# A second token mixer whose scores are laid over all four 64x64 tiles of the matmul array

## The chip, the cores and the metric

The kernel runs as one program on one core of a Trainium2 chip. The metric is the device time of one execution in microseconds (us). Engines are named as in the profile: PE is the matmul engine (TensorE), PEld its loading of weights, DVE is VectorE, ACT is ScalarE, POOL is GpSimd, SP starts most of the transfers. Each engine works through its own queue strictly in the order in which the program was laid out; a waiting instruction holds up everything behind it on its engine.

## The reference, cut to what matters

Two layers are computed for 256 frames of one prompt and 8 streams of 16 frames (samples). Each layer is SwiGLU block, token mixer, SwiGLU block, each followed by a layer norm. The change touches only the mixer of the second layer: grouped-query attention with 16 query heads, 4 key/value heads of 64 elements, rotary positions, and a learned "sink" per query head that takes part in the softmax as one more score without a value:

```python
def _attend(q, k, v, valid, bias, sinks):
    s = jnp.einsum("bqhgd,bkhd->bhgqk", q, k, ...) * (HEAD_DIM ** -0.5)
    ...
        sk = sinks.astype(jnp.float32)[None, :, :, None, None]
        m = jnp.maximum(jnp.max(s, axis=-1, keepdims=True), sk)
        e = jnp.exp(s - m)
        p = e / (jnp.sum(e, axis=-1, keepdims=True) + jnp.exp(sk - m))
    return jnp.einsum("bhgqk,bkhd->bqhgd", p.astype(v.dtype), v)
```

A prompt frame reads its own chunk of 64 frames and the two chunks before it; a sample frame reads 128 cached keys and the 16 of its own stream.

## The kernel before, in words

All activations stay in the core's memory, and the weights stream through a ring. A dense product in near-full precision is three matmuls (`mm3`, lines 193 to 195), high part times high part and two mixed ones. The second mixer (`mixer_b`) runs these stages: `m.natural` three times (the projections to the first half of the queries, to keys and values, to the second half of the queries), then `m.finish` (the output projection: 8 steps `k` of the contraction for each of 3 tiles `t` of frames, six dense matmuls each). The attention of 8 pairs of heads for the prompt (`prompt(c)`) and of 8 units of two streams (`sample(b, g)`) is cut into pieces by Python generators, and a small planner (`Flow`) puts the pieces between the dense matmuls. Each `yield` says how much PE time the piece costs, how long to wait before the next, which PSUM banks and buffers it keeps and which the next piece needs; `room` caps them. `finish` calls `flow.until(("p", k))` before it uses head pair `k`. Behind the planner a scheduler sets the final order of each engine's queue.

One unit of the prompt before: 8 score matmuls (line 983) with 64 rows of contraction and 64 columns of output, on the two tiles of the array that lie on its diagonal (row group r writes column group r); a softmax (reductions on DVE at line 991, exponentials on ACT at 994 and 999, scaling on DVE at 1005); six transposes (1011) copied out by ACT (`pTp`, 1014); four matmuls with v (1022); and ACT and DVE split the result into high and low parts (`xh`, `xl`, lines 71 and 72), from which the output projection reads it. One unit of the samples: four score matmuls (1037), softmax (1042 to 1058), four transposes (1062, 1064) copied out half by ACT (`pT`, 1068) and half by DVE (1069), eight matmuls with v (1078), and two copies to `oTs` (1084). The sinks are loaded once by four small transfers on POOL's queue (`load_sinks`, 875 and 878).

Of the kernel before, what the change touches and what calls it, by code (L numbers as in the profile page):

```python
# [45 lines left out]
def encoder_step(ctx, tc, a, o):  # L46
# [822 lines left out]
    def load_sinks():  # L869
        sinks = const.tile([P, 2], F32, name="sinksb")  # L870
        sinkp = const.tile([P, 8], F32, name="sinkpb")
        sk = a["sinks"]
        with nc.allow_non_contiguous_dma(reason="a few sinks"):
            for g in range(2):
                nc.gpsimd.dma_start(
                    sinks[:, g:g + 1], bass.AP(sk.tensor, sk.offset + 8 * g, [[1, 8], [0, DS], [1, 1]])
                )
                nc.gpsimd.dma_start(
                    sinkp[:, 4 * g:4 * g + 4],
                    bass.AP(sk.tensor, sk.offset + 8 * g, [[4, 2], [0, 64], [1, 4]]),  # L880
                )
        return sinks, sinkp
# [8 lines left out]
    def mixer_b(sunk, cache):  # L891
        with ExitStack() as st:
# [5 lines left out]
            nsinks = m.mp.tile([P, 2], F32, name="nsinksb")  # L898
            nc.vector.tensor_scalar(nsinks, sinks, -1.0, None, op0=ALU.mult)
            nsinkp = m.mp.tile([P, 8], F32, name="nsinkpb")  # L900
            nc.vector.tensor_scalar(nsinkp, sinkp, -1.0, None, op0=ALU.mult)


            sps = [m.mp.tile([P, 6 * P], F32, name=f"sp{i}b") for i in range(3)]
# [71 lines left out]
            def prompt(c):  # L976
                g = c // 4
                pks = [bank(), bank()]
                for u, (i, a0, a1, _) in enumerate(bands):
                    k0 = 64 if u == 3 else 0  # L980
                    for r in range(2):
                        w = slice(64 * r, 64 * r + 64)
                        nc.tensor.matmul(  # L983
                            pks[i][w, a0:a1], qT[w, c, 64 * u:64 * u + 64], kT[w, g, k0:k0 + a1 - a0],
                            start=True, stop=True,
                        )
                nm = stp.tile([P, 4], F32, name="nm4")
                sm = stp.tile([P, 4], F32, name="sm4")
                sp = sps[c % 3]
# [16 lines left out]
                yield 1.0, 3.82, {"bank": 2, "sp": 1}, {"bank": 2, "pTp": 1}  # L1006
                pT = m.m2.tile([P, 6, 2, 64], F32, name="pTp")
                for h, js in enumerate(((0, 1, 2, 4), (3, 5))):
                    pt = bank()
                    for i, j in enumerate(js):  # L1010
                        nc.tensor.transpose(  # L1011
                            out=pt[:, i * P:(i + 1) * P], in_=sp[:, j * P:(j + 1) * P], identity=ident
                        )
                    nc.scalar.copy(
                        pT[:, 4 * h:4 * h + len(js)].rearrange("p j r q -> p (j r q)"), pt[:, 0:len(js) * P]
                    )
                yield 0.65, 0.65, {"bank": 2, "pTp": 1}, {"bank": 1}
                po = bank()
                for t, js in enumerate((slice(0, 4), slice(4, 6))):
                    for r in range(2):  # L1020
                        w = slice(64 * r, 64 * r + 64)
                        nc.tensor.matmul(  # L1022
                            po[w, t * P:SEQ].rearrange("p (u q) -> p u q", q=64),
                            v[:, t, P * g + 64 * r:P * g + 64 * r + 64], pT[:, js, r, :],
                            start=(t == 0), stop=(t == 1),
                        )
                m.put_prompt(c, po[:, 0:SEQ])
# [3 lines left out]
            def sample(b, g):  # L1031

                pk = bank()[:, 0:2 * n].rearrange("p (i k) -> p i k", i=2)
                for i in range(2):
                    for r in range(2):
                        w = slice(64 * r, 64 * r + 64)
                        nc.tensor.matmul(  # L1037
                            pk[w, i, :], qs[w, g, b + i].rearrange("p j q -> p (j q)"), kc[w, b + i, g, :],
                            start=True, stop=True,
                        )  # L1040
                nm = stp.tile([P, 2], F32, name="nm")
                nc.vector.tensor_reduce(nm, pk, axis=AX.X, op=ALU.max, negate=True)
                nc.vector.tensor_scalar(nm, nm, nsinks[:, g:g + 1], None, op0=ALU.min)
                s = m.m3.tile([P, 2, n], F32, name="s")
                sm = stp.tile([P, 2], F32, name="sm")
                for i in range(2):
                    nc.scalar.activation(
                        s[:, i], pk[:, i], AF.Exp, bias=nm[:, i:i + 1], accum_out=sm[:, i:i + 1]
                    )
                es = stp.tile([P, 2], F32, name="es")  # L1050
                nc.scalar.activation(es, nm, AF.Exp, bias=sinks[:, g:g + 1])
# [7 lines left out]
                yield 0.5, 3.5, {"bank": 1, "s": 1}, {"bank": 1, "pT": 1}  # L1059
# [12 lines left out]
                for i in range(2):  # L1072
                    for l in range(2):
                        for r in range(2):
                            w = slice(64 * r, 64 * r + 64)
                            u = slice((2 * l + i) * P + 64 * r, (2 * l + i) * P + 64 * r + 64)
                            d = slice(P * g + 64 * r, P * g + 64 * r + 64)
                            nc.tensor.matmul(  # L1078
                                po[w, i, :], v[:, 2, d] if l else vc[:, b + i, d],
                                pT[:, u], start=(l == 0), stop=(l == 1),  # L1080
                            )
# [5 lines left out]
            def add_p(c):  # L1087
                flow.add({("k", 0), ("k", 1), ("q", 0, c), ("q", 1, c)}, {"bank": 2, "sp": 1}, prompt(c))

            def add_s(b, g):  # L1090
                flow.add({("k", 2)} | {("q", 2, 4 * g + j) for j in range(4)}, {"bank": 1, "s": 1}, sample(b, g))
# [153 lines left out]
```

## Time and profile before

| | us |
|---|---|
| median of 3 runs | 1419.72 (1419.4 to 1421.39) |
| profiled execution, its own time | 1419.12 |
| its span, from the first to the last instruction | 1417.4 |
| PE busy | 1404.8 (99%) |
| DVE busy | 1052.0 (74%) |
| ACT busy | 644.7 (45%) |
| POOL busy | 49.1 (3%) |

The span is what the trace covers; the execution's own time is 1.7 us longer. PE is busy nearly throughout, but matmuls overlap each other in the pipeline, so the length of a piece of PE work is read from the start of its first instruction to the start of what follows it, not from the sum of durations. The mixer's attention lies between about 1048 and 1125 us of the span.

### The profile page before, as it was taken

The page shows a single profiled execution, that of the slowest core. Times are in us where ns is not written, and L with a number is a line of the kernel's source. Part 1 is how long each engine was busy: PE and PEld are TensorE (multiplying, and loading weights), DVE is VectorE, ACT ScalarE, POOL GpSimd, SP SyncE. Part 2 cuts the span into 40 slices and gives each one's busy share as a digit, 9 for nine tenths or more (in the row PEclk, how much of TensorE's full clock was granted, in tenths as well). Part 3 has the DMA queues.
Part 4 walks back from the last instruction along what each step waited for, and adds up shares of the span by engine and source line. Part 5 has one row for each costly group of instructions (what it writes and reads, how often), then busy time and mean ns, then how long its engine had stood idle before and what let it go on. Part 6 is the DMA issues. An engine that isn't in the chain of part 4 may idle for free. (4 is left out here: it accounts for less than half of the span.)

```text
span 1417.4 us, 21251 instructions
## 1 busy us (share of the span) xinstructions
PE 1404.8 (99%) x8048; PEld 1270.9 (90%) x8048; DVE 1052.0 (74%) x1912; ACT 644.7 (45%) x1201; POOL 49.1 (3%) x72
## 2 busy tenths in 40 slices
PE   9999999999999999999999999999999999999997
PEld 8999999898887899999989999999787789999996
DVE  6877877755356787787777778786967788778775
ACT  6544444256564544444425444443346554444440
POOL 1110000100000000000000000000100000000001
PEclk9999999999999999999999999999999999999999
DMA  7645334375845543433425363433241164343321
GB/s 278 241 132 152 119 119 158 119 232 182 289 142 194 189 140 105 149 119 120 160 97 174 104 208 119 135 97 123 96 166 61 52 208 141 107 148 119 119 74 45
DMA packets 68693, 203.19 MB, mean 143 GB/s; under 512 B 6844, under 2 KB 19648, under 8 KB 68464
## 3 DMA queue, kind: packets, MB, share of 16 engines
q1 hardware_dynamic: 63344, 187.72, 39.7%
q0 software_dynamic: 2944, 10.71, 2.4%
q10 hardware_dynamic: 2304, 3.41, 0.6%
q8 instruction: 63, 1.03, 0.3%
q14 instruction: 38, 0.31, 0.1%
HBM read 196.56 MB, written 5.24 MB: 142 GB/s over the span
## 5 line engine op out<-in xcount | busy, mean ns | idle before, releaser
L193 PE MATMUL bank<-xh,ring_h 128*128 128x384 f32 x1440 | 486.5, 338 | 0.0
L195 PE MATMUL bank<-xh,ring_l 128*128 128x384 f32 x1440 | 483.5, 336 | 0.0
L194 PE MATMUL bank<-xl,ring_h 128*128 128x384 f32 x1440 | 482.4, 335 | 0.0
L72 DVE TENSOR_TENSOR ring_l<-raw,ring_h 128x1024 fp32r<-128x1024 f32 (+2 forms) x258 | 300.1, 1165 | 217.3 <-ACT ring_h L71 213.4
L71 ACT CAST ring_h<-raw 128x1024 fp32r<-128x1024 f32 (+2 forms) x258 | 258.2, 1003 | 400.4 <-PE bank L194 197.0
L193 PEld LDWEIGHTS bank<-xh,ring_h 128*128 128x128 f32 x1440 | 270.7, 188 | 8.7 <-issue 1.2
L194 PEld LDWEIGHTS bank<-xl,ring_h 128*128 128x128 f32 x1440 | 270.8, 188 | 6.7 <-DVE ring_l L72 0.5
L195 PEld LDWEIGHTS bank<-xh,ring_l 128*128 128x128 f32 x1440 | 270.5, 188 | 0.0
L71 ACT CAST ring_h<-wd 128x512 fp32r<-128x512 f32 x216 | 133.6, 619 | 103.4 <-PE bank L194 81.3
L371 DVE TENSOR_TENSOR x<-x,bank 128x512 f32<-128x512 f32 x236 | 160.5, 680 | 17.9 <-PE bank L195 16.9
L72 DVE TENSOR_TENSOR ring_l<-wd,ring_h 128x512 fp32r<-128x512 f32 x216 | 148.1, 686 | 13.8 <-ACT ring_h L71 13.8
L195 PE MATMUL bank<-ring_h,hl 128*128 128x512 f32 x348 | 137.6, 395 | 0.0
L193 PE MATMUL bank<-ring_h,hh 128*128 128x512 f32 x348 | 137.2, 394 | 0.0
L194 PE MATMUL bank<-ring_l,hh 128*128 128x512 f32 x348 | 136.8, 393 | 0.0
L193 PE MATMUL bank<-ring_h,xh 128*128 128x512 f32 x288 | 118.2, 410 | 0.0
L194 PE MATMUL bank<-ring_l,xh 128*128 128x512 f32 x288 | 113.3, 393 | 0.1
L195 PE MATMUL bank<-ring_h,xl 128*128 128x512 f32 x288 | 112.9, 393 | 0.0
L195 PEld LDWEIGHTS bank<-ring_h,hl 128*128 128x128 f32 x348 | 65.4, 188 | 15.7 <-DVE hl L72 0.8
L194 PEld LDWEIGHTS bank<-ring_l,hh 128*128 128x128 f32 x348 | 65.4, 188 | 12.5
L193 PEld LDWEIGHTS bank<-ring_h,hh 128*128 128x128 f32 x348 | 65.8, 189 | 11.9
L193 PEld LDWEIGHTS bank<-ring_h,xh 128*128 128x128 f32 x288 | 54.2, 188 | 13.8 <-issue 3.7
L195 PEld LDWEIGHTS bank<-ring_h,xl 128*128 128x128 f32 x288 | 54.1, 188 | 11.8 <-DVE xl L72 0.2
(195 smaller groups left out, 1425.6 us busy)
## 6 DMA issues: line engine op xcount, KB each, us to landing
raw<-in_w_in SPq DMA_DIRECT2D x172, 512.0 KB, 3.3
wd<-in_w_down SPq DMA_DIRECT2D x72, 512.0 KB, 4.3
raw<-in_w_down SPq DMA_DIRECT2D x16, 512.0 KB, 3.2
kta<-in_kT_a SPq DMA_DIRECT2D x16, 512.0 KB, 6.4
vca<-in_v_a SPq DMA_DIRECT2D x16, 512.0 KB, 6.9
raw<-in_w_qk_a SPq DMA_DIRECT2D x16, 512.0 KB, 3.7
raw<-in_w_qkv_b SPq DMA_DIRECT2D x12, 512.0 KB, 3.5
raw<-in_w_v_a SPq DMA_DIRECT2D x8, 512.0 KB, 4.2
```

The source lines that it names most:

```text
L71: cast = nc.scalar.copy(hi, src)
L72: nc.vector.tensor_tensor(lo, src, hi.bitcast(F32), op=ALU.subtract)
L193: nc.tensor.matmul(out, lh, rh, start=first, stop=False, skip_group_check=partial)
L194: nc.tensor.matmul(out, lh, rl, start=False, stop=False, skip_group_check=partial)
L195: nc.tensor.matmul(out, ll, rh, start=False, stop=last, skip_group_check=partial)
L371: nc.vector.tensor_tensor(z, z, sums[b], op=ALU.add)
```

## The change

Scores of the prompt are computed for two pairs of heads (c and c+1) in one piece, those of the samples for the two streams of a unit. For the second of the two, row group r of the array writes column group 1-r. So the four 64x64 tiles are all addressed, and the two score matrices go to different PSUM banks. The second one then has its heads' rows swapped, which is why sinks are loaded in both orders (16 small transfers for 4), why the sink's exponential of a sample takes an addition on DVE first, and why the matmuls with v read the swapped half (`r ^ x`). A piece of the prompt now holds four banks and two of four `sp` buffers, and the numbers that it tells the planner are others. `soften` is the softmax of one pair of heads as it was.

```diff
-                room = {"bank": 6, "sp": 3, "s": 3, "pTp": 2, "pT": 2, "qr": 2}
+                room = {"bank": 6, "sp": 4, "s": 3, "pTp": 2, "pT": 2, "qr": 2}
...
+                for i in range(2):
+                    for r in range(2):
+                        w = slice(64 * (r ^ i), 64 * (r ^ i) + 64)
+                        at = sk.offset + 8 * g + 4 * r
+                        nc.gpsimd.dma_start(sinks[w, g, i:i + 1], bass.AP(sk.tensor, at, [[1, 4], [0, DS], [1, 1]]))
+                        nc.gpsimd.dma_start(sinkp[w, g, :, i], bass.AP(sk.tensor, at + i, [[0, 64], [2, 2]]))
...
             def prompt(c):
                 g = c // 4
-                pks = [bank(), bank()]
+                pks = [[bank(), bank()] for _ in range(2)]
                 for u, (i, a0, a1, _) in enumerate(bands):
                     k0 = 64 if u == 3 else 0
...
+                    for x in range(2):
+                        for r in range(2):
+                            w, e = (slice(64 * q, 64 * q + 64) for q in (r, r ^ x))
+                            nc.tensor.matmul(
+                                pks[x][i][e, a0:a1], qT[w, c + x, 64 * u:64 * u + 64], kT[w, g, k0:k0 + a1 - a0],
+                                start=True, stop=True,
+                            )
+                for x in range(2):
+                    soften(c + x, pks[x])
+                yield 0.6, 6.0, {"bank": 4, "sp": 2}, {"bank": 2, "pTp": 2}
...
-                yield 1.0, 3.82, {"bank": 2, "sp": 1}, {"bank": 2, "pTp": 1}
...
-                yield 0.65, 0.65, {"bank": 2, "pTp": 1}, {"bank": 1}
+                yield 1.3, 0.65, {"bank": 2, "pTp": 2}, {"bank": 2}
...
             def sample(b, g):
-                pk = bank()[:, 0:2 * n].rearrange("p (i k) -> p i k", i=2)
+                pk = [bank()[:, 0:n] for _ in range(2)]
...
-                nc.vector.tensor_reduce(nm, pk, axis=AX.X, op=ALU.max, negate=True)
-                nc.vector.tensor_scalar(nm, nm, nsinks[:, g:g + 1], None, op0=ALU.min)
+                for i in range(2):
+                    nc.vector.tensor_reduce(nm[:, i:i + 1], pk[i], axis=AX.X, op=ALU.max, negate=True)
+                nc.vector.tensor_tensor(nm, nm, nsinks[:, g, :], op=ALU.min)
...
-                nc.scalar.activation(es, nm, AF.Exp, bias=sinks[:, g:g + 1])
+                nc.vector.tensor_tensor(es, nm, sinks[:, g, :], op=ALU.add)
+                nc.scalar.activation(es, es, AF.Exp)
...
-                yield 0.5, 3.5, {"bank": 1, "s": 1}, {"bank": 1, "pT": 1}
+                yield 0.25, 3.5, {"bank": 2, "s": 1}, {"bank": 1, "pT": 1}
...
-            for c in range(4):
+            for c in range(0, 4, 2):
                 add_s(2 * c, 0)
                 add_p(c)
+                add_s(2 * c + 2, 0)
             m.natural(512, take_q2, whole=True)
-            for c in range(4, 8):
+            for c in range(4, 8, 2):
                 add_p(c)
```

With the pieces' sizes the planner's order changes, and the two kernels' queues differ in three places that matter here. In the rows below a number behind a name tells one buffer from another; the sample units are called u1 to u8 and the prompt's head pairs p0 to p7, in the order in which their scores are computed.

PE before, at the tails of the last four sample units (`s_10294` and `s_10315` are the scores of u7 and u8):

```order
L193 MATMUL bank_10087<-ring_h_83,xh_81 128x512
L194 MATMUL bank_10087<-ring_l_84,xh_81 128x512
L195 MATMUL bank_10087<-ring_h_83,xl_82 128x512
L193 MATMUL bank_10088<-ring_h_83,xh_81 128x512
L194 MATMUL bank_10088<-ring_l_84,xh_81 128x512
L195 MATMUL bank_10088<-ring_h_83,xl_82 128x512
L1062 MATMUL bank_10384<-ident_73,s_10294 128x128
L193 MATMUL bank_10087<-ring_h_83,xh_81 128x512
L1062 MATMUL bank_10384<-ident_73,s_10294 128x128
L1064 MATMUL bank_10384<-ident_73,wideb_9192 128x128 x2
L194 MATMUL bank_10087<-ring_l_84,xh_81 128x512
L195 MATMUL bank_10087<-ring_h_83,xl_82 128x512
```

PE now, around the tail of the last sample unit (u8: `s_10026`, `pT_10135`), between the scores of p2 and p3 and their transposes (`sp2b`, `sp3b`):

```order
L986 MATMUL bank_10073<-kTb_9205,qTb_9206 64x192 x2
L1077 MATMUL bank_10130<-ident_73,s_10026 128x128 x2
L1079 MATMUL bank_10130<-ident_73,wideb_9208 128x128 x2
L1093 MATMUL bank_10138<-pT_10135,vcb_7727 64x64 x2
L999 MATMUL bank_10150<-ident_73,sp2b_9190 128x128
L1093 MATMUL bank_10138<-pT_10135,vb_9204 64x64 x2
L1093 MATMUL bank_10138<-pT_10135,vcb_7727 64x64 x2
L1093 MATMUL bank_10138<-pT_10135,vb_9204 64x64 x2
L999 MATMUL bank_10150<-ident_73,sp2b_9190 128x128 x3
L999 MATMUL bank_10156<-ident_73,sp2b_9190 128x128 x2
L999 MATMUL bank_10161<-ident_73,sp3b_9191 128x128 x4
L999 MATMUL bank_10167<-ident_73,sp3b_9191 128x128 x2
```

What moved: before, dense matmuls of the output projection stand between the steps of a sample unit. Now the projection's steps k=0 and k=1 for the first tile stand ahead of the tails of u2 to u8, and the next dense matmul comes after the matmuls with v of p2 and p3: from the transposes of u2 on, PE's queue holds 44 transposes, the scores of u5 to u8, of p2 with p3 and of p4 with p5, and the matmuls with v of u2 to u8, p2 and p3, and nothing else.

ACT before, where the copies `pT` of two sample units (`pT_9940`, `pT_9948`) stand beside the softmax of p3 (`sp0b_9176`):

```order
L1084 COPY oTsb_9169<-bank_9913 128x4x16 x2
L994 ACTIVATE sp0b_9176,sm4_9882<-bank_9871,nm4_9881 128x64
L994 ACTIVATE sp0b_9176,sm4_9882<-bank_9871,nm4_9881 128x128
L994 ACTIVATE sp0b_9176,sm4_9882<-bank_9871,nm4_9881 128x192
L994 ACTIVATE sp0b_9176,sm4_9882<-bank_9872,nm4_9881 128x192
L999 ACTIVATE es4_9892<-nm4_9881,sinkpb_2431 128x4
L1084 COPY oTsb_9169<-bank_9924 128x4x16 x2
L1068 COPY pT_9940<-bank_9935 128x256
L1068 COPY pT_9948<-bank_9943 128x256
```

ACT now, at the copy `pT` of u8 (`pT_10135`), which PE needs for u8's matmuls with v:

```order
L1029 ACTIVATE sp2b_9190,sm4_10091<-bank_10070,nm4_10090 128x64
L1029 ACTIVATE sp2b_9190,sm4_10091<-bank_10070,nm4_10090 128x128
L1029 ACTIVATE sp2b_9190,sm4_10091<-bank_10070,nm4_10090 128x192
L1029 ACTIVATE sp2b_9190,sm4_10091<-bank_10071,nm4_10090 128x192
L1034 ACTIVATE es4_10101<-nm4_10090,sinkpb_2431 128x4
L1029 ACTIVATE sp3b_9191,sm4_10111<-bank_10072,nm4_10110 128x64
L1029 ACTIVATE sp3b_9191,sm4_10111<-bank_10072,nm4_10110 128x128
L1029 ACTIVATE sp3b_9191,sm4_10111<-bank_10072,nm4_10110 128x192
L1029 ACTIVATE sp3b_9191,sm4_10111<-bank_10073,nm4_10110 128x192
L1034 ACTIVATE es4_10121<-nm4_10110,sinkpb_2431 128x4
L1083 COPY pT_10135<-bank_10130 128x256
```

What moved: two softmaxes, of p2 and p3, stand ahead of the copy, where one stood before.

ACT before, at the high part `xh` of p3's result (its matmuls with v wrote `bank_10044`), from which the output projection reads (`sp2b` is the softmax of p5, `sp0b` that of p6):

```order
L994 ACTIVATE sp2b_9178,sm4_10025<-bank_10015,nm4_10024 128x192
L999 ACTIVATE es4_10035<-nm4_10024,sinkpb_2431 128x4
L71 CAST xh_81<-bank_10044 128x2x128
L994 ACTIVATE sp0b_9176,sm4_10068<-bank_10057,nm4_10067 128x64
L994 ACTIVATE sp0b_9176,sm4_10068<-bank_10057,nm4_10067 128x128
```

ACT now, at the high parts of p2 and p3 (`bank_10231`, `bank_10232`), behind the softmaxes of p4 (`sp0b`) and p5 (`sp1b`):

```order
L1034 ACTIVATE es4_10202<-nm4_10191,sinkpb_2431 128x4
L1029 ACTIVATE sp1b_9189,sm4_10212<-bank_10173,nm4_10211 128x64
L1029 ACTIVATE sp1b_9189,sm4_10212<-bank_10173,nm4_10211 128x128
L1029 ACTIVATE sp1b_9189,sm4_10212<-bank_10173,nm4_10211 128x192
L1029 ACTIVATE sp1b_9189,sm4_10212<-bank_10174,nm4_10211 128x192
L1034 ACTIVATE es4_10222<-nm4_10211,sinkpb_2431 128x4
L71 CAST xh_81<-bank_10231 128x2x128
L71 CAST xh_81<-bank_10232 128x2x128
```

What moved: the high parts of two head pairs now come together, behind two softmaxes of the next two.

## Rows read from the trace of the kernel before

**Rows 1.** The page: busy us, share of the span, instructions of each engine.

```profile
PE 1404.8 (99%) x8048; PEld 1270.9 (90%) x8048; DVE 1052.0 (74%) x1912; ACT 644.7 (45%) x1201; POOL 49.1 (3%) x72
```

**Rows 2.** Windows: length, busy us (instructions) of PE, PEld, DVE, ACT, POOL, clock, DMA.

```profile
1048.00:1125.00 77.00, 75.13 (x642) 58.72 (x640) 54.52 (x202) 43.75 (x169) 2.21 (x4) 1.00 0.16 53
```

**Rows 3.** Timeline of PE: start, length, instructions, count [idle before, releaser].

```profile
1082.69 0.34 PE L1078 MATMUL bank<-pT,vcb 128*64 128x64 f32 x4
...
1083.77 0.44 PE L1062 MATMUL bank<-ident,s 128*128 128x128 f32 x2
...
1087.14 0.34 PE L1078 MATMUL bank<-pT,vb 128*64 128x64 f32 x4 [0.60 <-DVE pT L1069]
...
1091.25 0.87 PE L1022 MATMUL bank<-pTp,vb 128*64 128x256 f32 x8 [1.26 <-ACT pTp L1014]
...
1093.19 0.50 PE L193 MATMUL bank<-ring_h,xh 128*128 128x512 f32 x1
...
1100.15 0.82 PE L1011 MATMUL bank<-ident,sp1b 128*128 128x128 f32 x6
...
1101.56 1.52 PE L1022 MATMUL bank<-pTp,vb 128*64 128x256 f32 x16
```

**Rows 4.** Timeline of PE, scores of the prompt: three units together, one alone.

```profile
1048.80 3.17 PE L983 MATMUL bank<-kTb,qTb 64*64 64x64 f32 x48
1051.90 0.50 PE L193 MATMUL bank<-ring_h,xh 128*128 128x512 f32 x1
...
1092.06 1.20 PE L983 MATMUL bank<-kTb,qTb 64*64 64x64 f32 x16
```

**Rows 5.** Timeline of PE, scores of the samples: two units together.

```profile
1112.74 1.20 PE L1037 MATMUL bank<-kcb,qsb 64*64 64x144 f32 x16
```

**Rows 6.** Timeline of PE, the first mixer: matmuls on four column groups, two units.

```profile
338.00 1.12 PE L806 MATMUL bank<-kta,qbda 128*32 128x272 f32 x16
```

**Rows 7.** Timeline of ACT around 1085.

```profile
1081.60 0.38 ACT L1047 ACTIVATE s<-bank,nm 128x144 f32<-128x144 f32 x1 [1.63 <-DVE nm L1043]
...
1082.33 0.29 ACT L1051 ACTIVATE es<-nm,sinksb 128x2 f32<-128x2 f32 x1
...
1083.63 0.33 ACT L994 ACTIVATE sp0b<-bank,nm 128x64 f32<-128x64 f32 x1
...
1085.26 0.35 ACT L1084 COPY oTsb<-bank 128x64 f32<-128x64 f32 x2
1085.45 0.70 ACT L1068 COPY pT<-bank 128x256 f32<-128x256 f32 x2
...
1088.47 0.62 ACT L71 CAST xh<-oTsb 128x512 fp32r<-128x512 f32 x1
...
1090.61 0.86 ACT L1014 COPY pTp<-bank 128x512 f32<-128x512 f32 x2
```

**Rows 8.** Timeline of DVE around 1085.

```profile
1081.39 0.94 DVE L991 TENSOR_REDUCE nm<-bank 128x1 f32<-128x64 f32 x4
1082.65 0.16 DVE L1052 TENSOR_TENSOR sm<-sm,es 128x2 f32<-128x2 f32 x1 [0.32 <-ACT es L1051]
1082.73 0.22 DVE L992 TENSOR_SCALAR nm<-nm,nsinkpb 128x4 f32<-128x4 f32 x1
...
1083.59 0.23 DVE L1058 TENSOR_SCALAR wideb<-s,rc 128x16 f32<-128x16 f32 x1
...
1085.86 0.90 DVE L1005 TENSOR_SCALAR sp0b<-sp0b,rc 128x64 f32<-128x64 f32 x4
1086.67 0.75 DVE L1069 COPY pT<-bank 128x256 f32<-128x256 f32 x2
```

**Rows 9.** Timeline of POOL: the last transfer of sinks, and what follows it.

```profile
105.32 0.84 POOL L878 DMA_DIRECT2D sinkpb<-in_sinks  x1
266.75 0.93 POOL L231 TENSOR_TENSOR rstd<-ve,mhalf 128x1 f32<-128x1 f32 x1 [160.59 <-DVE ve L229]
```

**Rows 10.** The end of the span: PE's last matmul (timeline), then windows as in rows 2.

```profile
1409.42 0.39 PE L195 MATMUL bank<-ring_h,hl 128*128 128x512 f32 x1
```

```profile
1413.00:1415.00 2.00, 0.00 (x0) 0.00 (x0) 1.33 (x3) 0.00 (x0) 0.00 (x0) 0.63 0.24 88
```

More of the change, by code (lines that the diff above doesn't have):

```diff
@@ L869, in load_sinks @@
     def load_sinks():
-        sinks = const.tile([P, 2], F32, name="sinksb")
-        sinkp = const.tile([P, 8], F32, name="sinkpb")
+        sinks = const.tile([P, 2, 2], F32, name="sinksb")
+        sinkp = const.tile([P, 2, 2, 2], F32, name="sinkpb")
         sk = a["sinks"]
@@ L897, in mixer_b @@
             (sinks, sinkp), (kc, vc) = sunk, cache
-            nsinks = m.mp.tile([P, 2], F32, name="nsinksb")
+            nsinks = m.mp.tile([P, 2, 2], F32, name="nsinksb")
             nc.vector.tensor_scalar(nsinks, sinks, -1.0, None, op0=ALU.mult)
-            nsinkp = m.mp.tile([P, 8], F32, name="nsinkpb")
+            nsinkp = m.mp.tile([P, 2, 2, 2], F32, name="nsinkpb")
             nc.vector.tensor_scalar(nsinkp, sinkp, -1.0, None, op0=ALU.mult)
-            sps = [m.mp.tile([P, 6 * P], F32, name=f"sp{i}b") for i in range(3)]
+            sinkp, nsinkp = (t.rearrange("p g j i -> p (g j i)") for t in (sinkp, nsinkp))
+            sps = [m.mp.tile([P, 6 * P], F32, name=f"sp{i}b") for i in range(4)]
             for sp in sps:
@@ L977, in prompt @@
                 g = c // 4
-                pks = [bank(), bank()]
+                pks = [[bank(), bank()] for _ in range(2)]
                 for u, (i, a0, a1, _) in enumerate(bands):
                     k0 = 64 if u == 3 else 0
[L981 to L985, printed above, removed]
-                        )
+                    for x in range(2):
[5 more added lines that the diff above has]
+                            )
@@ new lines, in prompt @@
+                for x in range(2):
+                    soften(c + x, pks[x])
+                yield 0.6, 6.0, {"bank": 4, "sp": 2}, {"bank": 2, "pTp": 2}
+                pTs = []
+                for x in range(2):
+                    pT = m.m2.tile([P, 6, 2, 64], F32, name="pTp")
+                    for h, js in enumerate(((0, 1, 2, 4), (3, 5))):
+                        pt = bank()
+                        for i, j in enumerate(js):
+                            nc.tensor.transpose(
+                                out=pt[:, i * P:(i + 1) * P], in_=sps[(c + x) % 4][:, j * P:(j + 1) * P],
+                                identity=ident,
+                            )
+                        nc.scalar.copy(
+                            pT[:, 4 * h:4 * h + len(js)].rearrange("p j r q -> p (j r q)"), pt[:, 0:len(js) * P]
+                        )
+                    pTs.append(pT)
@@ new lines, in prompt @@
+                yield 1.3, 0.65, {"bank": 2, "pTp": 2}, {"bank": 2}
+                pos = [bank(), bank()]
+                for x in range(2):
+                    for t, js in enumerate((slice(0, 4), slice(4, 6))):
+                        for r in range(2):
+                            w = slice(64 * r, 64 * r + 64)
+                            nc.tensor.matmul(
+                                pos[x][w, t * P:SEQ].rearrange("p (u q) -> p u q", q=64),
+                                v[:, t, P * g + 64 * r:P * g + 64 * r + 64], pTs[x][:, js, r ^ x, :],
+                                start=(t == 0), stop=(t == 1),
+                            )
@@ L987, in prompt, with soften @@
+                for x in range(2):
+                    m.put_prompt(c + x, pos[x][:, 0:SEQ])
+            def soften(c, pks):
                 nm = stp.tile([P, 4], F32, name="nm4")
                 sm = stp.tile([P, 4], F32, name="sm4")
-                sp = sps[c % 3]
+                sp = sps[c % 4]
                 for u, (i, a0, a1, b0) in enumerate(bands):
@@ L1005, in prompt @@
                     nc.vector.tensor_scalar(sp[:, w], sp[:, w], rc[:, u:u + 1], None, op0=ALU.mult)
-                yield 1.0, 3.82, {"bank": 2, "sp": 1}, {"bank": 2, "pTp": 1}
[L1007 to L1016, printed above, removed]
-                yield 0.65, 0.65, {"bank": 2, "pTp": 1}, {"bank": 1}
[L1018 to L1027, printed above, removed]
             wide = m.wide()
             def sample(b, g):
-                pk = bank()[:, 0:2 * n].rearrange("p (i k) -> p i k", i=2)
+                pk = [bank()[:, 0:n] for _ in range(2)]
                 for i in range(2):
                     for r in range(2):
-                        w = slice(64 * r, 64 * r + 64)
+                        w, e = (slice(64 * q, 64 * q + 64) for q in (r, r ^ i))
                         nc.tensor.matmul(
-                            pk[w, i, :], qs[w, g, b + i].rearrange("p j q -> p (j q)"), kc[w, b + i, g, :],
+                            pk[i][e, :], qs[w, g, b + i].rearrange("p j q -> p (j q)"), kc[w, b + i, g, :],
                             start=True, stop=True,
@@ L1079, in sample @@
                                 po[w, i, :], v[:, 2, d] if l else vc[:, b + i, d],
-                                pT[:, u], start=(l == 0), stop=(l == 1),
+                                pT[:, u:u + 64], start=(l == 0), stop=(l == 1),
                             )
@@ L1087, in add_p @@
             def add_p(c):
-                flow.add({("k", 0), ("k", 1), ("q", 0, c), ("q", 1, c)}, {"bank": 2, "sp": 1}, prompt(c))
+                needs = {("k", 0), ("k", 1)} | {("q", t, c + x) for t in range(2) for x in range(2)}
+                flow.add(needs, {"bank": 4, "sp": 2}, prompt(c))
             def add_s(b, g):
-                flow.add({("k", 2)} | {("q", 2, 4 * g + j) for j in range(4)}, {"bank": 1, "s": 1}, sample(b, g))
+                flow.add({("k", 2)} | {("q", 2, 4 * g + j) for j in range(4)}, {"bank": 2, "s": 1}, sample(b, g))
             def take_q(t, acc):
```

11 lines of the change are left out of this document (2 added, 9 removed).

## Prediction

> **What bounds the kernel now.** First the page: PE is busy for 99% of the span, DVE for 74%, ACT for 45% [rows 1]. So what PE does not do is won, and what PE waits is lost, unless PE waits again behind it. Second the windows: over the mixer's attention, 1048 to 1125 us, PE is busy for 75.13 of 77.00 us at the full clock [rows 2]; 1.87 us are idle. Third the timeline of PE for these 1.87 us. They are two waits: 0.60 for DVE's copy `pT` and 1.26 for ACT's copy `pTp` [rows 3]. Both lie in the one stretch without dense matmuls, 1082.69 to 1093.19, 10.50 us [rows 3]. That is the pattern to keep in mind: dense matmuls hide the softmax on ACT and DVE, and where they are missing PE waits for copies that stand behind exponentials in a strict queue.
>
> **Gain 1, scores of the prompt.** Three units in a row take 1051.90 - 1048.80 = 3.10 us, 1.03 each; one alone takes 1093.19 - 1092.06 = 1.13, so going in and out costs some 0.10 [rows 3, 4]. One triple and five others are 3.10 + 5 x 1.13 = 8.75. If four tiles work at once, a pair of units takes what one takes: 4 x 1.13 = 4.5. Gain 4.2.
>
> **Gain 2, scores of the samples.** Two units take 1.13 us up to the next block (1.20 with the tail that overlaps it) [rows 5], 0.56 each, 4.5 for eight. Halved and entered alone each time, as the order has them: 8 x (0.28 + 0.10) = 3.0. Gain 1.5. Together 5.7. Bounds: 6.6 if every halving is whole and no entry costs anything (4.4 + 2.2), a loss of 0.8 if nothing overlaps and eight sample units pay their own entry.
>
> Do four tiles work at once? Row and column groups mixed are in no row. Nearest is the first mixer: 16 instructions of 272 columns on four column groups, each with a moving operand of its own, take 1.12 us [rows 6]. One after another, at the 0.117 us that a 128-column transpose takes (twelve from 1100.15 to 1101.56 [rows 3]), they would take 16 x 0.117 x 272/128 = 4.0. So four streams run side by side. Likewise a prompt unit on two row groups has 2304 columns of instructions (four each of 64, 128, 192 and 192), 2.1 us at that rate, and takes 1.03 [rows 4]. Each half of the new pattern is there; I take the whole.
>
> **Gain 3.** The two waits, 1.9 us, lose their places in the new order. What is late instead comes next.
>
> **Loss 1, the stretch S.** After the change the dense matmuls that stood between the tails of the sample units are gone (order of PE, first place). S runs from the transposes of u2 to the matmuls with v of p2 and p3. Loads of the three queues in S, from rows:
> - PE: 44 transposes x 0.117 = 5.1; scores of four sample units 4 x 0.38 = 1.5; seven sample units with v at (1083.77 - 1082.69)/2 = 0.54, 3.8; two pairs of prompt scores 2.3; p2 and p3 with v 1.4. Sum 14.1 [rows 3].
> - ACT: seven `pT` x 0.35 = 2.5; fourteen `oTs` at 0.35 for two, 2.4; four sample softmaxes from 1081.60 to 1082.62, 1.02 each, 4.1; two prompt softmaxes from 1083.63 to 1085.26, 1.63 each, 3.3; two `pTp` pairs at 0.86, 1.7; three casts or copies of 512 columns at 0.62, 1.9. Sum 15.9 [rows 7].
> - DVE: seven `pT` x 0.38 = 2.6; reductions of four sample units, two each at the 0.24 of one of four, 1.9; their minimum and the added sink 4 x (0.22 + 0.16) = 1.5; sum, reciprocal and scaling of four units from 1082.65 to 1083.82, 1.17 each, 4.7, and 0.8 of a fifth; two low parts at 0.62, 1.2; p2 and p3 2 x (0.94 + 0.22 + 0.4 + 0.90) = 4.9. Sum 17.6 [rows 8].
>
> So the softmax engines have more to do than PE, and every unit passes back and forth between the three. In the stretch of before, ACT had 8.4 us of such work (three prompt softmaxes 4.9, eight `oTs` 1.4, two `pT` 0.7, a cast 0.6, a `pTp` pair 0.9) in 10.50, filled to 0.80 [rows 3, 7]. At that share S lasts 17.6/0.80 = 22.0 and PE idles 7.9. Walking the three queues in the new order with the same prices and 0.1 for each hand-over, I get 24.4 and these waits of PE: u5's scores for its queries 0.9; u4 with v for `pT` 1.1; u5 and u6, transposes and with v, in small pieces 2.4; u7 with v 1.6, since its `pT` stands behind u8's exponentials; and u8 with v 4.2. The last is the clearest (order of ACT, second place): `pT` of u8 stands behind the softmaxes of p2 and p3, which start only when their scores are done, on PE just ahead. That is 0.94 + 0.22 on DVE, 2 x 1.63 + 0.35 on ACT, less 0.5 of transposes that PE has meanwhile. In before the same copy stood behind one softmax, already running. Sum 10.2. I take 9 for S, between the two, nearer to the walk since it is of this order. Bounds 3.5 (S as short as DVE's load) and 11.
>
> **Loss 2, behind S.** The first dense matmul there writes a bank that p4's exponentials still read: 0.94 + 0.22 + some 1.2 for three of four, less 1.4 of matmuls with v: 0.9. The projection's step k=2 needs `xh` of p2, behind the softmaxes of p4 and p5 (third place of the order): 1.3 beyond the ten dense matmuls ahead of it, at (1100.15 - 1093.19)/30 = 0.23 [rows 3]. The transposes of p6 and `xh` of p4 wait likewise behind p7: 0.8. Sum 3.0, bounds 0.5 and 5. **Loss 3, ahead of S:** u1 with v behind the `pTp` copies of p0 and p1, 1.2, bounds 0 and 2. In every case what queues behind the waiting matmul is the projection, and behind it the rest of the kernel, dense to its end, so nothing gives it back.
>
> **Costed at nothing.** Twelve more transfers of sinks at 0.84 take POOL some 10 us at 105 us; POOL then idles for 160.59 [rows 9]. If that cover were gone, the layer norm behind would be late by as much. Three more memsets on POOL, idle in that stage (2.21 of 77 us [rows 2]). The swapped indices change no count on PE.
>
> **The sum.** -5.7 - 1.9 + 9 + 3 + 1.2 = +5.6 on the profiled execution's 1419.12 gives 1424.7. The median of the runs is 0.6 above that execution, so 1425.3.
>
> **Rivals.**
> - The tiles do not mix (chance 0.12): the eight scores cost as before plus 0.8: -1.9 + 13.2 + 0.8 = +12.1, 1431.8. For it: no row shows the mix. Against it: both halves of it do.
> - The clock falls (0.14). At the end of the span PE stops at 1409.8, and the mean clock of 1413 to 1415 is 0.63 of full: full speed for 0.26 of these 2 us, half after, so it went from 2.4 to 1.2 GHz at 1413.5, 3.7 us after the last matmul [rows 10]. The hold at u8 is longer, in a stretch where PE is little busy. If it falls there, the 4.3 us of PE work left in S take as long again: 1429.6. Against it: in before no wait of that length shows what a clock does between two pieces of work.
> - S lasts as long as its busier reader (0.08): PE and ACT are then always ready for DVE, S is 17.6 with 3.5 idle, 5.5 less than I take: 1419.8. Against it: in before's stretch the busiest was filled to 0.80 only [rows 3, 7]. The Trainium skill has this as a rule against the change: "Tiling speeds up TensorE but not PSUM evacuation", so that the copying becomes the bottleneck (TensorEngine Tiling (Array Packing), Performance Considerations, PSUM Bottleneck). Read strictly it gives this rival; by rows 3 and 7 the engines wait for each other too.
> - The handing over is no worse than before (0.12), the case on the other side. In before's stretch PE idled 1.86 of 10.50, a share of 0.18 [rows 3]. The mechanism: the softmaxes of p0, p1 and u1 to u4 are done under the 48 dense matmuls ahead, the rest stays one unit ahead of PE, and scores end sooner. Then S lasts 14.1/0.82 = 17.2 with 3.1 idle, Losses 2 and 3 hide under dense matmuls, and -5.7 - 1.9 + 3.1 = -4.5 gives 1415.2. It decides as soon as all added idle is under 7.6 us. Against it: DVE alone has 17.6 to do, and the hold at u8 follows from the queue.
>
> The Trainium skill makes a rule of the clock rival: half clock is the default, and activity releases it (TensorE: Matmul & The Clock Gate, Part 1). Rows 10 agree for the fall; no run so far shows the way back within the mixer.
>
> **How the numbers follow.** My forecast has 0.54. Its own range is 1419 to 1430 by the bounds of S. The whole one, 1418 to 1433, takes in the mixed-tile rival and the clock, and leaves out the best case and two mishaps at once. A measurement here can tell about 0.2%, 2.8 us. Faster by more, below 1416.9: most of the last rival, 0.10. Within: the rest of it, the third (0.08) and the low tail of the forecast, together 0.15. Slower, above 1422.6: 0.75.
>
> **What would show it.** Gain 1: a pair of prompt scores takes 1.1 us to the next block, not 2.1. Gain 2: a sample unit 0.4, not 0.56. PE's busy time falls by some 6 us, while its idle time in the mixer rises from 1.9 to some 13, with ACT's copy `pT` first among those waited for and one wait of about 4 us just ahead of the transposes of p2. The clock stays at 1.00 over the mixer, or the second rival is right. Less than 6 us idle there, or a longest wait under 2 us, would prove me wrong on S; scores at the old price would prove me wrong on the tiles.

## The result, and the profile after

The changed kernel takes 1430.01 us (median of 6 runs, 1429.01 to 1431.09), the kernel before 1419.93 beside it: ratio 1.0071, 95% interval 1.0061 to 1.0082. It is slower, as forecast and inside the range, but by 10.1 us where the sum had 5.6.

Where the time arose: from the first scores of the prompt to the first transpose of the block behind the mixer, before took 1150.62 - 1048.80 = 101.82 us and after takes 1160.88 - 1048.94 = 111.94. From there to the last matmul both need 259.2. So all of it lies in the mixer. That first transpose, in before and in after (timelines of PE):

```profile
1150.62 0.38 PE L399 MATMUL bank<-ident,hf 128*128 128x128 f32 x2
```

```profile
1160.88 0.38 PE L399 MATMUL bank<-ident,hf 128*128 128x128 f32 x2
```

The page after, its line of busy times (answers to [rows 1]):

```profile
PE 1405.6 (98%) x8048; PEld 1270.6 (89%) x8048; DVE 1053.9 (74%) x1928; ACT 644.1 (45%) x1201; POOL 56.3 (4%) x87
```

The page hardly shows it: PE's busy time is nearly the same (1405.6 for 1404.8), since work done at half speed counts as busy for twice as long. The windows of after do (length, busy us of PE, PEld, DVE, ACT, POOL, then the clock); the first one answers to [rows 2] and is 10 us longer, the second is the stretch S of the prediction:

```profile
1048.00:1135.00 87.00, 75.49 (x640) 57.87 (x639) 55.82 (x217) 43.82 (x173) 2.41 (x4) 0.94 0.21 71
1081.41:1108.35 26.94, 20.10 (x269) 14.65 (x267) 18.22 (x92) 15.70 (x74) 0.00 (x0) 0.87 0.01 2
1058.00:1060.00 2.00, 1.75 (x11) 1.18 (x12) 1.09 (x7) 0.00 (x0) 0.43 (x2) 0.55 0.00 0
1060.00:1062.00 2.00, 2.00 (x7) 1.59 (x6) 1.02 (x6) 0.93 (x5) 0.00 (x0) 0.60 0.00 0
...
1098.00:1100.00 2.00, 0.00 (x0) 0.00 (x0) 0.97 (x6) 2.00 (x12) 0.00 (x0) 0.79 0.02 4
1100.00:1102.00 2.00, 0.73 (x5) 0.48 (x5) 1.65 (x10) 1.21 (x6) 0.00 (x0) 0.50 0.00 0
1102.00:1104.00 2.00, 2.00 (x18) 1.80 (x18) 0.48 (x3) 0.93 (x4) 0.00 (x0) 0.50 0.00 0
1104.00:1106.00 2.00, 2.00 (x24) 1.67 (x26) 0.69 (x1) 1.63 (x5) 0.00 (x0) 0.51 0.00 0
1106.00:1108.00 2.00, 2.00 (x38) 1.40 (x32) 1.39 (x8) 0.08 (x2) 0.00 (x0) 1.00 0.00 0
```

PE is idle for 87.00 - 75.49 = 11.51 us where it was idle for 1.87. And the clock is at half, 1.2 GHz, in two stretches: 3.4 us from 1058.2 ((1 - 0.55) x 2 / 0.5 = 1.8, and 1.6 likewise) and 6.8 us from 1099.2. The first is nearly all work, so half of it, 1.7 us, is the price; in the second PE works from 1101.27 on, 4.7 us, price 2.35.

What PE waits for (us in total, times, longest), the first five groups of after's view of waits:

```profile
PE bank L1093 <- ACT pT L1083: 6.3, 5, 4.2
PE bank L1050 <- POOL kcb L947: 3.5, 1, 3.5
PE bank L1156 <- DVE warm L1153: 1.5, 1, 1.5
PE bank L839 <- ACT ob L836: 1.1, 2, 0.5
PE bank L193 <- ACT sp0b L1029: 0.8, 1, 0.8
```

(The third and fourth lie outside the second mixer.) The same in the timeline of PE in after, which answers to [rows 3 to 5]: a pair of prompt scores, the scores of u1, sample scores in S, the hold at u8, and the first dense matmul behind S:

```profile
1048.94 1.22 PE L986 MATMUL bank<-kTb,qTb 64*64 64x64 f32 x32
1050.08 0.50 PE L193 MATMUL bank<-ring_h,xh 128*128 128x512 f32 x1
...
1058.25 0.76 PE L1050 MATMUL bank<-kcb,qsb 64*64 64x144 f32 x8 [3.51 <-POOL kcb L947]
...
1084.75 0.48 PE L1050 MATMUL bank<-kcb,qsb 64*64 64x144 f32 x8
1085.16 0.44 PE L1077 MATMUL bank<-ident,s 128*128 128x128 f32 x2
...
1101.27 0.48 PE L1093 MATMUL bank<-pT,vcb 128*64 128x64 f32 x4 [4.16 <-ACT pT L1083]
...
1109.14 0.50 PE L193 MATMUL bank<-ring_h,xh 128*128 128x512 f32 x1 [0.79 <-ACT sp0b L1029]
```

The four tiles work: a pair of head pairs takes 1.14 us to the next block, what one took before (1.13), and a sample unit 0.41 instead of 0.56. The hold at u8 is 4.16 us, forecast at 4.2. The hold of 3.51 at u1 stood in no term. Its cause on ACT and POOL, in two more timelines of after:

```profile
1052.58 1.28 ACT L1029 ACT_TABLE_LOAD   x1 [2.52 <-DVE nm L1027]
1053.87 0.32 ACT L1029 ACTIVATE sp0b<-bank,nm 128x64 f32<-128x64 f32 x1
...
1057.11 0.40 ACT L940 COPY kTb<-bank 128x256 f32<-128x256 f32 x1
```

```profile
1057.57 0.86 POOL L947 COPY kcb<-kTb 128x128 f32<-128x128 f32 x2 [7.17 <-ACT kTb L940]
```

The samples' new keys are copied from PSUM by ACT (`keys`, line 940) and then by POOL into `kc`, which u1's scores read. ACT's copy stands behind the loading of the exponential's table and the softmaxes of p0 and p1. In before this chain ended later still, at 1068.5, but the first scores of the samples came only at 1071.63 (timeline of POOL in before):

```profile
1067.87 0.67 POOL L946 COPY kcb<-kTb 128x128 f32<-128x128 f32 x2 [17.61 <-ACT kTb L939]
```

### The profile page after: what moved, and what is told of

It is laid out like the page before. It is cut to its first block, busy times and chain, and to the rows that moved or that the text cites. A ratio compares the mean times of both kernels' runs of the same rounds, so it can differ in the third digit from the quotient of the medians.

```text
span 1427.7 us, 21271 instructions
## 1 busy us (share of the span) xinstructions
PE 1405.6 (98%) x8048; PEld 1270.6 (89%) x8048; DVE 1053.9 (74%) x1928; ACT 644.1 (45%) x1201; POOL 56.3 (4%) x87
```

## The experiments

Times are medians; "against before" is the ratio with its 95% interval. From here on "mixer" is the time from the first prompt scores to the first transpose behind the mixer, in the profiled execution (101.82 before, 111.94 changed). "Less than the changed kernel" is a difference of medians; as the intervals are about 0.1% to either side, such a difference of under some 2 us is not clear of noise by itself.

**e1, the keys first.** The copy goes ahead in ACT's queue:

```diff
-                nc.scalar.copy(
-                    kT[:, :, t * P:(t + 1) * P], pt[:, 0:2 * P].rearrange("p (g q) -> p g q", q=P)
-                )
+                with tc.high_priority(offset=80 if t == 2 else 0):
+                    nc.scalar.copy(
+                        kT[:, :, t * P:(t + 1) * P], pt[:, 0:2 * P].rearrange("p (g q) -> p g q", q=P)
+                    )
```

> As the changed kernel, but ACT's copy of the new sample keys (kT of token tile 2, L940) is put ahead of most of p0's exponentials. Theory (the wait is a place in ACT's queue): POOL's copy kcb comes some 3 us earlier, the PE wait of 3.51 us at the scores of u1 falls to 1 us or less, the clock does not fall there (windows 1058 to 1062 at 1.00, some 1.7 us of work at half speed given back), p0's softmax ends 0.4 later; sum about -4.5 us, 1425.5 (ratio to the kernel before 1.004). Rival (the wait only moves: PE then waits for softmaxes of p0 and p1, which end no sooner): within 1.5 us of the changed kernel, 1429 to 1430.

Measured 1426.82, against before 1.0050 (1.0037 to 1.0062): 3.2 us less than the changed kernel. The wait at u1 fell, and the half clock behind it went (timeline of PE, then a window of e1):

```profile
1054.61 0.48 PE L1051 MATMUL bank<-kcb,qsb 64*64 64x144 f32 x8 [0.89 <-POOL kcb L948]
```

```profile
1058.00:1060.00 2.00, 2.00 (x11) 1.65 (x10) 1.96 (x10) 0.00 (x0) 0.00 (x0) 1.00 0.00 0
```

So the wait is a place in ACT's queue. 1.3 us of the expected 4.5 are missing. The profiled execution is the longest of the five (1424.64 to 1429.22), and its mixer, 112.20, is no shorter than the changed kernel's: u1's matmuls with v now wait 1.71 for `pT` (0.34 in after), which stands on ACT behind a cast that waits 1.27 for a transfer of weights, and the clock fell at 1072.8, 1093.3 and 1100.1, in and ahead of the sparse stretch.

```profile
1071.39 0.34 PE L1094 MATMUL bank<-pT,vcb 128*64 128x64 f32 x4 [1.71 <-ACT pT L1084]
```

So the trace shows what the copy's place does to the wait; that time is won rests on the medians alone.

**e2, the same order on two tiles.** Both halves of every pair on the diagonal, at the five places where `r ^ x` or `r ^ i` stood, as here:

```diff
-                            w, e = (slice(64 * q, 64 * q + 64) for q in (r, r ^ x))
+                            w = e = slice(64 * r, 64 * r + 64)
```

> The changed kernel's order, instruction for instruction on PE and ACT, but both halves of every pair lie on the two diagonal tiles, so that two tiles work and not four. Theory (four tiles work side by side): a pair of prompt scores goes from 1.14 to 2.1 us, a sample unit from 0.40 to 0.56 or more; PE's busy time rises by 4 to 6 us, part of it inside waits that shrink; about +4 us against the changed kernel, 1434 (ratio 1.010). Rival (the four tiles give nothing, the order alone made the difference): pair and unit as long as in the changed kernel, time within 1 us of its 1430.

Measured 1433.04, against before 1.0095 (1.0081 to 1.0109), 3.0 us more than the changed kernel. The timeline of PE in e2, for the same two kinds of scores:

```profile
1048.68 2.19 PE L986 MATMUL bank<-kTb,qTb 64*64 64x64 f32 x32
1050.80 0.50 PE L193 MATMUL bank<-ring_h,xh 128*128 128x512 f32 x1
...
1057.76 0.71 PE L1050 MATMUL bank<-kcb,qsb 64*64 64x144 f32 x8 [2.32 <-POOL kcb L947]
1058.40 0.50 PE L193 MATMUL bank<-ring_h,xh 128*128 128x512 f32 x1
```

2.12 to the next block instead of 1.14, and 0.64 instead of 0.40 (a sample unit of the changed kernel at full clock). At these prices four tiles save 4 x 0.98 + 8 x 0.24 = 5.8 us of PE's work, but only 3.0 of time (2.9 in the mixers). PE is idle for 8.66 us in e2's window and for 11.51 in the changed kernel's, so the other 2.85 are waited away:

```profile
1048.00:1135.00 87.00, 78.34 (x628) 61.24 (x627) 53.32 (x212) 43.93 (x172) 1.16 (x3) 0.94 0.18 59
```

The new order without the four tiles costs 13 us against before.

**e3, the copies first; e4, both.** The two copies `pT` of a sample unit go ahead in their queues, alone (e3) and with e1's edit (e4):

```diff
+                with tc.high_priority(offset=80):
-                nc.scalar.copy(pT[:, 0:2 * P], pt[:, 0:2 * P])
-                nc.vector.tensor_copy(pT[:, 2 * P:], pt[:, 2 * P:])
+                    nc.scalar.copy(pT[:, 0:2 * P], pt[:, 0:2 * P])
+                    nc.vector.tensor_copy(pT[:, 2 * P:], pt[:, 2 * P:])
```

> The changed kernel, but the two copies pT of every sample unit (L1083, L1084) go to the front of their queues as soon as they are ready to be placed: pT of u8 stands behind one exponential of p2, not behind both softmaxes of p2 and p3. Theory (the hold of 4.16 us is a place in the queue, and the half clock from 1099 to 1106 follows from it): PE waits under 1 us at u8 with v, but then 2 to 3 us for the softmaxes of p2 at the transposes sp2b, since they end no sooner; the clock falls less; about -3 us, 1427. Optimist's rival (the whole hold and the half clock go): -6 us, 1424. Pessimist's rival (everything moves on to sp2b): within 1 us of 1430.

> Both edits, the keys first and the copies pT first. Theory (two separate waits in two places): the gains add up, about -7.5 us against the changed kernel, 1422.5, still not faster than the kernel before by 0.2%. Rival (one wait feeds the other, since a later u1 also moves p2 and p3): clearly less than the sum of the two single edits.

e3: 1426.44, against before 1.0046 (1.0032 to 1.0060), 3.6 less than the changed kernel. The long hold splits as the theory has it (timeline of PE in e3):

```profile
1096.98 0.34 PE L1094 MATMUL bank<-pT,vcb 128*64 128x64 f32 x4 [1.24 <-ACT pT L1084]
...
1099.12 1.00 PE L999 MATMUL bank<-ident,sp2b 128*128 128x128 f32 x6 [1.11 <-DVE sp2b L1040]
1100.76 1.51 PE L999 MATMUL bank<-ident,sp3b 128*128 128x128 f32 x6 [0.64 <-ACT pTp L1003]
```

4.16 became 1.24 + 1.11 + 0.64: the softmaxes end no sooner. e4: 1422.35, against before 1.0020 (1.0011 to 1.0029), 7.7 less than the changed kernel where the single gains add up to 6.8, the same within the noise. The two waits are separate.

**e5, only the samples.** The kernel before with the change's sample units.

> The kernel before with the change's sample units alone (four tiles, two banks instead of one, its sinks); prompt heads one by one as before. Theory (the price comes from the pairs of prompt heads, which claim four of the planner's six banks): Gain 2 shows, 8 x (0.56 - 0.40) = 1.3 us, and the order stays nearly that of before: 1418.3, no wait of PE over 1.5 us. Rival (a second bank for each sample unit is enough to disturb the planner): 1421 or more, with waits of PE at sample units.

1419.39, against before 0.9996 (0.9987 to 1.0005): no difference. The gain of 1.3 does not show in the time, but no wait is over 0.9 in the mixer either, so neither expectation holds whole. In the trace the gain is there: the samples' scores take 3.1 us in all up to the next block instead of 4.6. But the prompt's scores, cut into more pieces by other work, take 9.6 instead of 8.8, and PE idles 0.3 more. So the price does not come from the samples by themselves, and their gain goes largely into the pieces around them.

**e6, the claims.** Why does S hold no dense matmul? The planner's `fits` adds what all units hold to what a step asks for. In the changed kernel p0 with p1 holds four banks and u1 two, together the six of `room`. Neither's next step, which asks for two or one more, fits, nor do the transposes of the queries, which ask for one. So the planner puts nothing but dense matmuls until `until` forces it: in after they stand from 1050.08 to 1071.21, with only u1's scores and a transpose of the keys between. Those are missing later. The edit:

```diff
-                yield 0.6, 6.0, {"bank": 4, "sp": 2}, {"bank": 2, "pTp": 2}
+                yield 0.6, 6.0, {"bank": 4, "sp": 2}, {"pTp": 2}
-                yield 1.3, 0.65, {"bank": 2, "pTp": 2}, {"bank": 2}
+                yield 1.3, 0.65, {"bank": 2, "pTp": 2}, {}
-                yield 0.25, 3.5, {"bank": 2, "s": 1}, {"bank": 1, "pT": 1}
+                yield 0.25, 3.5, {"bank": 2, "s": 1}, {"pT": 1}
-                yield 0.45, 0.7, {"bank": 1, "pT": 1}, {"bank": 1}
+                yield 0.45, 0.7, {"bank": 1, "pT": 1}, {}
```

> The changed kernel, with only the planner's claims of banks changed: a unit that holds banks no longer asks for further ones for its next step (prompt pair: 4 held + 2 asked for, sample: 2 + 1; six in all). Theory (with p0 and p1 holding four and u1 two, no step fits into six any more, the planner puts 16 us of dense matmuls there and none is left for S): dense matmuls stand between the tails again, the hold of 4.16 at u8 and the half clock behind it go; the wait of 3.51 for the keys and its half clock stay: some 5.5 us of idle and 2.4 of half clock less, 1422. Rival (S is the load of DVE and ACT, whatever stands between): idle time of PE in the mixer stays over 9 us, 1427 or more.

1424.93, against before 1.0035 (1.0022 to 1.0048), 5.1 less than the changed kernel; the theory's 8 is missed. The mechanism holds: PE's idle time in the window 1048 to 1135 is 6.88, the hold at u8 is gone, and 3.46 of the rest is the keys' wait, which the edit left. But behind that wait the clock stood at half for 6.8 us instead of 3.4, and it fell again at 1095.9, behind a wait of 1.83 for `xh` (line 193).

```profile
1048.00:1135.00 87.00, 80.12 (x661) 59.93 (x660) 60.75 (x224) 45.87 (x177) 2.41 (x4) 0.94 0.15 51
```

**e8 and e9, a better order, on four tiles and on two.** e6's claims and e1's copy, and:

```diff
-                room = {"bank": 6, "sp": 4, "s": 3, "pTp": 2, "pT": 2, "qr": 2}
+                room = {"bank": 7, "sp": 4, "s": 3, "pTp": 2, "pT": 2, "qr": 2}
-                yield 0.6, 6.0, {"bank": 4, "sp": 2}, {"pTp": 2}
+                yield 0.6, 5.0, {"bank": 4, "sp": 2}, {"pTp": 2}
-                yield 1.3, 0.65, {"bank": 2, "pTp": 2}, {}
+                yield 1.3, 1.0, {"bank": 2, "pTp": 2}, {}
-                yield 0.45, 0.7, {"bank": 1, "pT": 1}, {}
+                yield 0.45, 1.4, {"bank": 1, "pT": 1}, {}
-                add_s(2 * c, 0)
                 add_p(c)
-                add_s(2 * c + 2, 0)
+            for b in range(0, DB, 2):
+                add_s(b, 0)
```

> The changed kernel with the claims of e6, the keys' copy first as in e1, seven banks for the planner instead of six, p0 to p3 entered ahead of the samples, and three waiting times of the planner (6.0 to 5.0, 0.65 to 1.0, 0.7 to 1.4). Theory: both long waits and both falls of the clock go; against the changed kernel some 9 us of idle time and 4 of half clock less: 1417, down to 1414 if every small wait goes too; that is faster than the kernel before, since the gains of the four tiles (some 5.9) now stand against less than 3 us of added waits. Rival (the softmax engines bound the stretch): not under the 1419.6 of the kernel before.

> The order of e8, instruction for instruction on PE and ACT, with two tiles at a time instead of four. Theory (where little is waited for, the four tiles are worth their whole price: 4 pairs x 0.98 + 8 sample units x 0.24 = 5.8 us): 5 to 6 us slower than e8. Rival (as between the changed kernel and its diagonal twin, part of the gain hides in waits): 3 us slower.

e8: 1416.80, against before 0.9981 (0.9972 to 0.9989), the fastest of all, though by just 0.2%. Its window, and three lines of its waits of PE, the longest in the mixer's attention:

```profile
1048.00:1135.00 87.00, 84.57 (x701) 63.90 (x700) 68.71 (x234) 50.69 (x185) 3.00 (x5) 1.00 0.25 84
```

```profile
PE bank L1051 <- POOL kcb L948: 0.8, 1, 0.8
PE bank L1051 <- ACT qsb L970: 0.8, 1, 0.8
PE bank L1078 <- DVE s L1073: 0.6, 1, 0.6
```

The clock stays full, 2.43 us are idle, the mixer takes 99.25. How much each of the edits beyond those of e6 and e1 brings is not separated. e9: 1420.59, against before 1.0003 (0.9994 to 1.0012), 3.8 slower than e8. That lies between the two expectations. e9 idles only 1.33 us, so 1.1 of the 5.8 is waited away even here. The rest of what is missing lies in e8's scores: its fourth pair took 1.46, not 1.14 (0.2 of it waiting for a bank that ACT's copy to `xh` still read), and its sample units lie between 0.4 and 0.8, so all scores together take some 4.7 us less than in e9 and not 5.8. The window of e9:

```profile
1048.00:1135.00 87.00, 85.67 (x685) 65.92 (x686) 66.02 (x230) 49.27 (x181) 3.00 (x5) 1.00 0.22 75
```

**e10 and e11, the hold filled.** The clock's price by itself: useless matmuls (cached v, 256 columns, against the identity) ahead of u8's matmuls with v, 16 in e10, 9 in e11; the trace counts two for each:

```diff
+                po = bank()
+                if (b, g) == (DB - 2, 1):
+                    fill(po[:, 256:512], 9)
+                po = po[:, 0:P].rearrange("p (i m) -> p i m", i=2)
```

> The changed kernel with 16 useless matmuls of 256 columns (some 3 us) in PE's queue just ahead of u8's matmuls with v, where PE stood idle for 4.16 us; the copy pT that it waits for stays where it is. Theory (the half clock from 1099.14 to 1105.97 is the price of the idle hold, apart from the hold itself): the wait ends at the same time, but the clock stays at 1.00 there, and the 4.7 us of work done at half speed take 2.35: 2.3 us off the changed kernel, 1427.7; the first fall at 1058.18 stays. Rival (the clock falls for the sparse stretch as a whole, not for the hold): no gain, 1430 or more.

> As e10, but 9 useless matmuls instead of 16: in e10 they took 7.07 us (0.44 each, not the 0.18 that was assumed), 2.7 us more than the hold. Nine take 4.0, just inside the hold of 4.16. Theory (half clock follows the idle hold): the copy pT is still what ends the wait, the clock stays at 1.00 from 1096 to 1106, and 2.3 us come back against the changed kernel: 1427.7. Rival (e10 showed full clock only because PE was kept busy for 7 us; the sparse work around the hold would bring the clock down all the same): 1429.5 to 1430.5.

e10: 1430.34, against before 1.0072 (1.0058 to 1.0085), no gain, and inconclusive as made: the 16 took 7.07 us, far past the hold, yet the clock stayed full there (timeline of PE in e10).

```profile
1097.75 7.07 PE L1046 MATMUL bank<-vcb,ident 128*128 128x256 f32 x32
```

e11: 1427.64, against before 1.0056 (1.0042 to 1.0070), as expected to 0.1. Timeline of PE and windows of e11, at the place where after stood at half clock:

```profile
1096.38 4.05 PE L1046 MATMUL bank<-vcb,ident 128*128 128x256 f32 x18
1100.70 0.34 PE L1100 MATMUL bank<-pT,vcb 128*64 128x64 f32 x4 [0.27 <-ACT pT L1087]
```

```profile
1100.00:1102.00 2.00, 1.73 (x22) 1.08 (x22) 1.58 (x8) 0.81 (x6) 0.00 (x0) 1.00 0.00 0
1102.00:1104.00 2.00, 2.00 (x43) 1.75 (x41) 0.70 (x2) 1.97 (x7) 0.00 (x0) 1.00 0.00 0
1104.00:1106.00 2.00, 1.74 (x24) 0.99 (x16) 1.96 (x10) 1.02 (x7) 0.00 (x0) 1.00 0.04 8
```

PE waits for the same copy until the same moment (52.2 us behind the first prompt scores, 52.3 in after) and does no more useful work. Only the clock differs, and the mixer takes 109.79, 2.15 less than in after. That the median agrees so well is partly luck: the five executions lie between 1425.41 and 1429.25, with mean granted clocks of 0.999 to 0.996, so how long the clock stood at half differs from one to the next, and the interval of the ratio overlaps that of the changed kernel. In the traces, then, the hold is paid twice: by its length, and by the half-speed work behind it.

## Why the direction was right and the size was not

The direction came out right because the added idle time outgrew the gain in work, as forecast. Two steps failed: Loss 3, which did not ask what u1 reads, and the clock, which the sum put at nothing.

- Gain 1 and Gain 2, per piece right: 1.14 against 1.13 forecast, 0.41 against 0.38. In sum they came to less. The mixer's 111.94 less 11.51 idle less 4.05 of half clock is 96.4 us of work, before 101.82 - 1.87 = 99.95: 3.55 gained, 5.7 forecast. Of the missing 2.15 some 1.4 is seen in the scores themselves: of the four pairs one was split into 0.47 and 1.02 by other work and one took 1.44 (0.2 of it waiting for a bank that ACT's copy to `pTp` still read); of the sample units u3 took 0.73, and u8 was split into 0.38 and 0.40. For the rest no run was made, and the cause is open.
- Gain 3 was right: neither of the two old waits is left.
- Loss 1 was right in its main mechanism. The hold at u8, 4.2 forecast and 4.16 measured, stood where the order of ACT put it; e3 shows the cause. The walk's other waits, 6.0, came to 2.7: 6.84 idle where it had 10.2 and I took 9. The length agrees by luck: the walk gave 24.4 us for S, and it lasted 26.94, of which 2.35 is half clock, 24.6; but PE worked 17.7 us where 14.1 were counted from single prices.
- Loss 2 was too large: 0.79 for the bank that p4's exponentials read (forecast 0.9), and nothing for `xh` of p2 or behind p7. 3.0 forecast, 0.8 measured.
- Loss 3 failed in its mechanism. "u1 with v behind the `pTp` copies", 1.2, bounds 0 and 2: that wait was 0.34. But the scores of u1, two steps earlier, waited 3.51 for the keys, above the bound. I had followed PE and ACT from u1's result on and not what u1 reads. In before's trace POOL's copy caused no wait, because nothing needed it yet; moving a reader ahead made it late.
- The clock. The second rival had the mechanism, "the hold at u8 is longer", with 1429.6 and a chance of 0.14. The fall came there and at u1's wait as well: 1.7 + 2.35 in place of 4.3 at one place, and e11 shows the second of the two by itself. The term at nothing was 4.05 us, most of the 4.5 by which the forecast was short. The sign "The clock stays at 1.00 over the mixer, or the second rival is right" came out for the rival; that its time is met to 0.4 us is luck, since its one fall of 4.3 stands for two.

Together: forecast were -5.7 of work, -1.9 + 9 + 3 + 1.2 = +11.3 of idle time and nothing for the clock, 5.6; measured are -3.55, +9.64 and +4.05, 10.1, which is what the mixer shows. The idle time was overrated by 1.7 and the gain in work by 2.15; without the clock the sum would have been +6.1, near the forecast because these two errors cancel. What made the result worse than the forecast is the clock. The sign that PE's busy time falls by some 6 us did not show, since the half-speed work filled it up again. What was costed at nothing did cost nothing: POOL is done with the sinks at 117.45 and then idles 149.15 us, and the first prompt scores stand at 1048.94, before at 1048.80.

Of the other rivals: the tiles mix (e2, 2.12 against 1.14). That S lasts as long as its busier reader is excluded by the windows, since DVE is busy for 18.22 of 26.94. The Trainium skill's rule that "Tiling speeds up TensorE but not PSUM evacuation" (TensorEngine Tiling (Array Packing), Performance Considerations, PSUM Bottleneck) fits in part; the Trainium skill says there only that the copying may become the bottleneck. Of 5.8 us saved on PE, 3.0 reached the time in the changed order and 3.8 in e8's. Over S, though, neither engine that reads PSUM was full (DVE 18.22 us, ACT 15.70 of 26.94); the two long waits came from the order of ACT's queue (e1, e3). "The handing over is no worse than before" failed here; e8, with 2.43 us idle, comes near it, 1416.8 where that rival gave 1415.2; it took another set of claims and another order to get there.

## What to carry to other kernels

Follow every operand of a unit that moves ahead, through all engines that make it, and not only what comes behind its result. If a planner counts buffers, add up what the units hold and what their next steps ask for: at a sum just over the room it stops, and the filler that should hide later waits is spent early. And price a hold like the 3.51 and 4.16 us here as its length plus the work behind it that may run at half speed. Filling the hold gave the second part back (e11).

## What the runs showed of the hardware

Four 64x64 tiles, with two moving streams on each row group, overlap fully: the 16 matmuls of a pair (the trace counts 32) took 1.14 us to the next block on four tiles and 2.12 on the two diagonal ones. Full clock came back within the mixer both times in after, at 1061.6 and 1106.0, while PE worked on. The Trainium skill's rule that activity releases the clock (TensorE: Matmul & The Clock Gate, Part 1) agrees with that; before had no row on it. With every idle hold of 3.46 us or more the clock fell, during it or at its end (after, e1, e2, e3, e6, e10, e11), and stayed at half for 3.4 us in some cases and 6.8 in others. It also fell without such a hold: in e3 and e4 behind waits of 1.24 and 1.11, in e6 behind 1.28 and 1.83, in e1 at 1072.8 behind one of 1.71 and at 1093.3 and in e2 at 1094.2 behind waits of at most 0.9. The hold of 2.32 in e2, the waits up to 0.8 in e8 and the 1.26 of before brought no fall. What decides it is left open; filling the hold (e10, e11) kept the clock full at that place. A single-precision matmul of 256 columns took 0.44 us over the whole array, not the 0.18 that I had read off the matmuls with v, which lie on half of it two at a time.
